# Five RMS norms of a decoder step: one product of ones and a root on 272 columns in place of small sums, small roots and a spread

## The chip, the cores and the metric

The kernel runs on one core of a Trainium2 chip. A core has a matmul engine (TensorE, PE in the profile; its weight loads are shown as PEld), three engines for elementwise work (VectorE = DVE, ScalarE = ACT, GpSimd = POOL), and queues that start DMAs (SP's, ACT's and POOL's). Each engine works through its own queue in order; semaphores hold an instruction until what it reads is there and what it overwrites is free. The metric is the device time of one execution, in microseconds (us).

## What is computed

One layer of a hybrid decoder, for a prompt of 512 tokens and 32 sample tokens (8 sequences of 4), 544 tokens in all, with a model width of 1024, in float32. With the parts that matter here spelled out:

```
def _rmsnorm(x, g):
    return x * rsqrt(mean(x * x, axis=-1) + 1e-6) * g

def _layer(x, ...):
    m = mixer(_rmsnorm(x, norm_mix_pre), ...)       # RG-LRU and attention branches, then @ W_out
    x = x + _rmsnorm(m, norm_mix_post)
    f = conv_ffn(_rmsnorm(x, norm_ffn_pre), ...)    # @ W_up, conv over 3 positions, gelu gate, @ W_down
    x = x + _rmsnorm(f, norm_ffn_post)
```

## The kernel before

The activations lie turned: a tile holds 128 channels on its partitions and the tokens along its columns, so the width of 1024 is eight tiles (index c), and a sum over the width is a sum over partitions and over eight tiles. The tokens come in two halves, of 272 and 272 columns (HALF2) up to the FFN's start and of 256 and 288 (HALF) in the down projection. Half a = 0 is worked on first.

Each float32 operand of a large product is split into a high and a low part (names ending in H and L, weights wh and wl), and a product is made of three matmuls for each 128 channels. ScalarE writes the high parts, VectorE subtracts for the low parts. The weights are split as they arrive (wh_e, wl_e for the first FFN products).

A norm in the middle of the kernel, in norm_chain(a, acc), goes like this. While a projection's tiles come out of PSUM, ScalarE squares them and VectorE adds the squares up in one tile acc of [128 channels, 272 tokens]. Then:

- stats: acc itself is loaded as weights, in three pieces of 128 columns, against a single column of ones. The result, a PSUM tile pst with one token on each partition and three columns, holds the sums. newton_rstd takes the root of it on ScalarE (AF.Sqrt from a table), the reciprocal and one Newton step on VectorE, all on 3 columns.
- diag: VectorE multiplies the identity by each of the three columns, which gives diagonal tiles (dg).
- spread: a product of ones [128 x 128] with dg puts each token's factor on all 128 partitions (PSUM tile rep, 272 columns).
- then, for each c, VectorE multiplies the tile by its gain (a column of pv) and by rep.

This is done for the norm behind the out-projection (tiles named ..._m0 and ..._m1) and, once x1 = x + that norm and its squares (accx) are there, for the norm ahead of the FFN (..._f0, ..._f1). The normalised tiles are then split into b11, b21 (half 0) and b12, b22 (half 1), the operands of the FFN's first products (pq). The last norm, finish_b ("o1"), does the same for the second half of the FFN's output ft; its squares lie in two tiles, acc and sq7, so there are six small products. Token tiles 0 and 1 of the output take another way, with tokens on partitions: newton_rstd on one column (rstd), and for tile 1 a root written out at the kernel's end.

The order of the work. TensorE's order is that of the program, throughout. A clock `now` counts steps of products: half of an out-projection or one FFN product is 0.5. A generator started with start_at runs until its next `yield t` and goes on t later on that clock; what it emits then stands behind the products emitted so far. NORM_TICKS, YS, YA, YB and FB are such pauses: YS between the sums and diag, YA and YB between diag and spread, NORM_TICKS between the first norm's work and the sums of the second, FB ahead of the spread in finish_b. For VectorE, ScalarE and POOL the order is written out by hand too, except between the end of the mixer and the FFN's main loop (some 370 to 450 us), where a scheduler orders them by priority and readiness; norm_chain raises the priority there (tc.high_priority). In the last stage ScalarE's and VectorE's order is again that of the program, and POOL's is not.

ScalarE's functions come from tables. A one-element activation (warm) ahead of a stage makes the table load happen early: at the kernel's start, at the end of the mixer (L1153) and near the end of the down projection (L1926).

Of the kernel before, what the change touches and what calls it, by code (L numbers as in the profile page):

```python
# [56 lines left out]
NORM_TICKS = (3.5, 1)  # L57
# [3 lines left out]
YA = (0.5, 0.5)  # L61
YB = (0.5, 0.5)
EARLY = 4
PLAIN = 6
FB = (1.0,)
# [58 lines left out]
def hawk_step(ctx, tc, I, O):  # L124
# [249 lines left out]
    act.activation(warm, epst, AF.Sqrt)  # L374
# [27 lines left out]
    pv = keep.tile([P, 96], F32, name="pv")  # L402

# [10 lines left out]
    G_PRE, G_POST, G_FPRE, G_FPOST, C_W, C_B, C_BR, C_BI, C_LAM = 0, 8, 16, 24, 32, 64, 72, 80, 88  # L414
# [738 lines left out]
    act.activation(warm, epst, AF.Sqrt)  # L1153
# [3 lines left out]
    def stats(acc, nch, nm, more=None):  # L1157

        ps = PX("pst_" + nm)
        for z in range(nch):  # L1160
            mm(ps[:, z:z + 1], acc[:, z * P:(z + 1) * P], ones[:, 0:1], z == 0, more is None and z == nch - 1)
        for z in range(nch if more is not None else 0):
            mm(ps[:, z:z + 1], more[:, z * P:(z + 1) * P], ones[:, 0:1], False, z == nch - 1)
        st = SM("nst_" + nm, [P, 3, 4], "nst")
        v, r, s_ = (st[:, z, :nch] for z in range(3))
        newton_rstd(r, v, s_, ps[:, :nch])
        return r

    def diag(r, n, nm):
        dg = T("dg_" + nm)  # L1170
        for z in range((n + P - 1) // P):
            w = min(P, n - z * P)
            dve.tensor_scalar(dg[:, z * P:z * P + w], ident[:, :w], r[:, z:z + 1], None, ALU.mult)
        return dg

    def spread(dg, n, nm):

        rep = PX("rep_" + nm)
        mm(rep[:, :n], ones, dg[:, :n], True, True)
        return rep  # L1180

    def sq_sum(acc, src, n, first, nm):
        if first:
            act.activation(acc[:, :n], src, AF.Square)
            if n % P:
                pool.memset(acc[:, n:n + P - n % P], 0.0)
# [53 lines left out]
    def norm_chain(a, acc):  # L1240
        lo, hi = HALF2[a]
        n = hi - lo
        nch = (n + P - 1) // P
        with tc.high_priority(offset=HP):
            r = stats(acc, nch, f"m{a}")
            yield YS[a]
            dg = diag(r, n, f"m{a}")
        yield YA[a]
        with tc.high_priority(offset=HP):
            rep = spread(dg, n, f"m{a}")  # L1250
# [6 lines left out]
            for c in range(0 if a else 8):  # L1257
                m_ = mt[c][:, lo:hi]
                stt(m_, m_, pv[:, G_POST + c:G_POST + c + 1], rep[:, :n], ALU.mult, ALU.mult)
                pool.tensor_tensor(out=x1_(c), in0=x1_(c), in1=m_, op=ALU.add)  # L1260
                sq_sum(acc2, x1_(c), n, c == 0, f"x{a}_{c}")
            for g in range(6 if a else 0):
                for c in range(2 * g, 2 * g + 2) if g < 4 else ():
                    m_ = mt[c][:, lo:hi]
                    stt(m_, m_, pv[:, G_POST + c:G_POST + c + 1], rep[:, :n], ALU.mult, ALU.mult)
                    pool.tensor_tensor(out=x1_(c), in0=x1_(c), in1=m_, op=ALU.add)
                for c in range(2 * g - 3, 2 * g - 1) if 1 <= g < 6 else ():
                    if 0 <= c < 8:
                        sq[c] = acc2 if c == 0 else T(f"sq_x{a}_{c}")
                        act.activation(sq[c][:, :n], x1_(c), AF.Square)  # L1270
                        if c == 0 and n % P:
                            pool.memset(acc2[:, n:n + P - n % P], 0.0)
# [4 lines left out]
        with tc.high_priority(offset=HP):  # L1277
            r = stats(acc2, nch, f"f{a}")
            yield YS[a]
            dg = diag(r, n, f"f{a}")  # L1280
        yield YB[a]
        with tc.high_priority(offset=HP):
            rep = spread(dg, n, f"f{a}")

            def normed(c, dst):
                stt(dst, x1[c][:, lo:hi], pv[:, G_FPRE + c:G_FPRE + c + 1], rep[:, :n], ALU.mult, ALU.mult)
# [521 lines left out]
    def finish_b(acc):  # L1808
# [3 lines left out]
        dg = diag(stats(acc, 3, "o1", sq7), n, "o1")  # L1812
        yield FB[0]
        rep = spread(dg, n, "o1")
        for c in range(8):
            f_ = ft[c][:, lo:hi]
            stt(f_, f_, pv[:, G_FPOST + c:G_FPOST + c + 1], rep[:, :n], ALU.mult, ALU.mult)
# [103 lines left out]
    for c in range(8):  # L1921
# [3 lines left out]
        if c == 5:  # L1925
            act.activation(warm, epst, AF.Sqrt)  # L1926
# [35 lines left out]
    act.activation(s_, ssq[:, 1, 2:3], AF.Sqrt, scale=1.0 / D, bias=b_)  # L1962
# [4 lines left out]
    dve.reciprocal(r, s_)  # L1967
# [40 lines left out]
```

## Time and profile before

| | us |
|---|---|
| three runs | 977.36, 978.94, 979.18 (median 978.94) |
| profiled execution | 977.74 |
| its span in the profile | 976.0 |
| granted TensorE clock | 0.998 of full speed |
| busy in the span | PE 967.6, PEld 959.9, DVE 758.6, ACT 551.0, POOL 168.8 |

The span lies inside the execution's time: 1.74 us are outside it. A busy TensorE isn't TensorE at its peak, since matmuls overlap and their ends are modelled. The chain that ended last, followed back from the end of the span, tells which engine's work set the end.

### The profile page before, as it was taken

The numbers are of one execution on the slowest core, as the hardware profiler recorded it, in microseconds if no ns is written. First come the engines' busy times: TensorE is split into PE (matmuls) and PEld (weight loads), VectorE is DVE, ScalarE is ACT, GpSimd is POOL, SyncE is SP. The second block draws the span as 40 slices with busy tenths as digits, with TensorE's granted clock in tenths as the row PEclk, the third lists the DMA queues.
The fourth block names the chain that finished last, engine by engine and source line by source line (L and its number), as shares of the span: only waits on it lengthen the run. The fifth ranks groups of instructions, "written<-read, shape, count | busy, mean of one in ns | idle before, by whom it ended". The sixth has DMA issues, their size and how long they took to land.

```text
span 976.0 us, 20122 instructions
## 1 busy us (share of the span) xinstructions
PE 967.6 (99%) x7668; PEld 959.9 (98%) x7668; DVE 758.6 (78%) x1632; ACT 551.0 (56%) x1344; POOL 168.8 (17%) x288
## 2 busy tenths in 40 slices
PE   9999999999999999999999999999999999999997
PEld 8999999999999999999999999999999999999996
DVE  5777888857858555699967888787888888888875
ACT  6544443467476435556767665655555555556652
POOL 2152000003306331230011111101011101011024
PEclk9999999999999999999999999999999999999999
DMA  7875535632334547136157585858586766768612
GB/s 217 237 239 163 151 88 147 161 93 87 109 113 126 175 121 189 45 122 184 39 114 189 126 191 129 184 137 177 140 179 157 169 156 160 166 140 221 201 30 92
DMA packets 234204, 143.07 MB, mean 147 GB/s; under 512 B 25012, under 2 KB 218940, under 8 KB 234076
## 3 DMA queue, kind: packets, MB, share of 16 engines
q1 hardware_dynamic: 224300, 120.21, 43.9%
q0 software_dynamic: 9696, 19.42, 11.9%
q10 hardware_dynamic: 112, 2.17, 0.6%
q8 instruction: 60, 0.98, 0.4%
q14 instruction: 36, 0.29, 0.1%
HBM read 115.59 MB, written 15.17 MB: 134 GB/s over the span
## 4 chain that ended last, share of the span: by engine, by line
PE 97%; DVE 1%; ACT 1%; DMA 0%; issue 0%; SPq 0%; POOL 0%; ACTq 0%; POOLq 0%
PE pmin L165 20%; PE pmdn L165 19%; PE pux L1536 16%; PE puy L1536 8%; PE pq L1536 7%; PE pmout L165 5%; PE pmlo L165 5%; PE pmao L165 5%; PE puz L1536 4%; PE pg L165 1%; PE pvp L165 1%; PE psc L165 1%; PE ptok L165 1%; DMA pt<-pd 0%; PE ps_warm L165 0%; PE pm_first L165 0%
## 5 line engine op out<-in xcount | busy, mean ns | idle before, releaser
L165 PE MATMUL pmin<-hH,wh_in 128*128 128x256 f32 (+1 forms) x568 | 164.0, 291 | 0.0
L165 PE MATMUL pmin<-hL,wh_in 128*128 128x256 f32 (+1 forms) x568 | 162.5, 288 | 0.0
L165 PE MATMUL pmin<-hH,wl_in 128*128 128x256 f32 (+1 forms) x568 | 159.3, 288 | 0.0
L165 PE MATMUL pmdn<-fH,wh_dn 128*128 128x256 f32 (+1 forms) x448 | 129.3, 289 | 0.0
L165 PE MATMUL pmdn<-fH,wl_dn 128*128 128x256 f32 (+1 forms) x448 | 129.2, 288 | 0.0
L165 PE MATMUL pmdn<-fL,wh_dn 128*128 128x256 f32 (+1 forms) x448 | 129.0, 288 | 0.0
L165 PEld LDWEIGHTS pmin<-hH,wh_in 128*128 128x128 f32 x568 | 107.3, 189 | 1.2 <-issue 1.0
L165 PEld LDWEIGHTS pmin<-hL,wh_in 128*128 128x128 f32 x568 | 107.4, 189 | 0.1
L165 PEld LDWEIGHTS pmin<-hH,wl_in 128*128 128x128 f32 x568 | 104.8, 188 | 0.2 <-issue 0.2
L177 DVE SCALAR_TENSOR_TENSOR uc<-u,fv,uc 128x560 f32<-128x560 f32 x128 | 102.0, 797 | 1.7 <-ACT uc L1567 1.1
L165 PEld LDWEIGHTS pmdn<-fL,wh_dn 128*128 128x128 f32 x448 | 84.4, 188 | 0.0
L165 PEld LDWEIGHTS pmdn<-fH,wl_dn 128*128 128x128 f32 x448 | 84.4, 188 | 0.0
L165 PEld LDWEIGHTS pmdn<-fH,wh_dn 128*128 128x128 f32 x448 | 84.4, 188 | 0.0
L1664 ACT COPY u<-pux 128x272 f32<-128x272 f32 x52 | 20.1, 386 | 84.4 <-PE pux L1536 84.2
L168 DVE TENSOR_TENSOR u<-puy,u 128x240 f32<-128x240 f32 (+2 forms) x78 | 24.6, 343 | 48.8 <-PE puy L1536 32.2
L174 DVE TENSOR_TENSOR ft<-ft,pmdn 128x256 f32<-128x256 f32 (+1 forms) x104 | 45.0, 434 | 15.7 <-PE pmdn L165 15.7
L283 ACT ACTIVATE wh_in<-raw_in 128x512 fp32r<-128x512 f32 x70 | 42.2, 625 | 20.7 <-issue 11.0
L290 DVE TENSOR_TENSOR wl_in<-raw_in,wh_in 128x512 fp32r<-128x512 f32 x70 | 47.8, 694 | 1.0 <-ACT wh_in L283 1.0
L1567 ACT ACTIVATE uc<-u,fv 128x560 f32<-128x560 f32 x64 | 48.2, 755 | 0.0
L779 ACT ACTIVATE s<-s,st 128x256 f32<-128x256 f32 (+1 forms) x32 | 15.2, 475 | 53.8 <-DVE st L776 46.1
L168 DVE TENSOR_TENSOR wl_dn<-raw_dn,wh_dn 128x512 fp32r<-128x512 f32 x56 | 38.3, 685 | 3.8 <-ACT wh_dn L1485 3.8
L1474 POOL DMA_DIRECT2D raw_up_s<-raw_up_s x26 | 22.4, 861 | 95.8 <-DMA raw_up_s<-raw_up__11277 5.4
(761 smaller groups left out, 3388.5 us busy)
## 6 DMA issues: line engine op xcount, KB each, us to landing
raw_in<-in_w_in_dram SPq DMA_DIRECT2D x35, 512.0 KB
raw_dn<-in_w_down_dram SPq DMA_DIRECT2D x56, 256.0 KB
raw_up_s<-in_w_up_dram SPq DMA_DIRECT2D x25, 512.0 KB
raw_up_s<-raw_up_s POOLq DMA_DIRECT2D x26, 256.0 KB, 5.3
raw_ao<-in_w_attn_o_dram SPq DMA_DIRECT2D x8, 512.0 KB
raw_lo<-in_w_lru_o_dram SPq DMA_DIRECT2D x8, 512.0 KB
raw_out<-in_w_out_dram SPq DMA_DIRECT2D x8, 512.0 KB
pd<-pb SPq DMA_DIRECT2D x12, 256.0 KB
```

The lines of the kernel that those rows point to most:

```text
L165: pe.matmul(out, l, r, start=start, stop=stop)
L168: dve.tensor_tensor(out=out, in0=a, in1=b, op=ALU.subtract)
L174: dve.tensor_tensor(out=out, in0=a, in1=b, op=ALU.add)
L177: dve.scalar_tensor_tensor(out=out, in0=a, scalar=s_, in1=b, op0=op0, op1=op1)
L283: act.activation(hl[0], raw, AF.Copy)
L290: (eng or dve).tensor_tensor(out=hl[1], in0=raw, in1=f32(hl[0]), op=ALU.subtract)
L779: act.activation(s3[:, j, :], s3[:, j, :], AF.Exp, bias=ng[:, j:j + 1], accum_out=sm[:, j:j + 1])
L1474: pool.dma_start(out=w["p4"], in_=w["p2"], accum_op=ALU.add)
L1536: pe.matmul(ps[:, :HN], w, x, start=start and k == 0 and i == 0, stop=stop and k == 3 and i == 2, skip_group_check=True)
L1567: act.activation(yt[j][:, 0:FLATU], u[:, 0:FLATU], AF.Copy, scale=fv[:, j:j + 1])
L1664: act.copy(e[nm_], z)
```

## The change

All five norms of the middle and the end (m0, m1, f0, f1, o1) take one way: a product of ones [128 x 128] with the tile of squares puts the sum of each token on all 128 partitions at once (272 columns, 288 at the end, where the two tiles of squares are accumulated). ScalarE takes the reciprocal root of it from a table (Abs_reciprocal_sqrt) on all columns and squares it; VectorE makes a Newton step in two multiplications on all columns, whose result is -2 times the factor and is left in the same PSUM tile. The gains are multiplied by -0.5 once, at the start (pvn). The Newton steps on few columns (the first norms, token tiles 0 and 1) take the same table function and lose their reciprocal. POOL's zeroing of the columns beyond 272 goes. The pauses YA and YB go, NORM_TICKS[0] rises from 3.5 to 4, so that the second product of half 0 stands where its sums stood; for half 1 a pause of 0.5 is kept between root and Newton step; FB falls from 1.0 to 0.5.

```diff
-NORM_TICKS = (3.5, 1)
+NORM_TICKS = (4, 1)
 YS = (0.5, 0.5)
-YA = (0.5, 0.5)
-YB = (0.5, 0.5)
-FB = (1.0,)
+FB = (0.5,)
...
-    act.activation(warm, epst, AF.Sqrt)
+    act.activation(warm, epst, AF.Abs_reciprocal_sqrt)
...
     def newton_rstd(r, v, s_, sq):
-        act.activation(s_, sq, AF.Sqrt, scale=1.0 / D, bias=epst)
+        act.activation(r, sq, AF.Abs_reciprocal_sqrt, scale=1.0 / D, bias=epst)
         dve.tensor_scalar(v, sq, 1.0 / D, EPS, ALU.mult, ALU.add)
-        dve.reciprocal(r, s_)
...
+        dve.tensor_scalar(pvn, pv[:, 8:32], -0.5, None, ALU.mult)
...
-    def stats(acc, nch, nm, more=None):
-        ps = PX("pst_" + nm)
-        for z in range(nch):
-            mm(ps[:, z:z + 1], acc[:, z * P:(z + 1) * P], ones[:, 0:1], ...)
...
-        newton_rstd(r, v, s_, ps[:, :nch])
-    def diag(r, n, nm):
...
-    def spread(dg, n, nm):
-        rep = PX("rep_" + nm)
-        mm(rep[:, :n], ones, dg[:, :n], True, True)
+    def total(accs, n, nm):
+        ps = PX("pst_" + nm)
+        for z, acc in enumerate(accs):
+            mm(ps[:, :n], ones, acc[:, :n], z == 0, z == len(accs) - 1)
+        return ps
+
+    def root_table(ps, n, nm):
+        y, w = (T(f"{x}_{nm}")[:, :n] for x in ("ry", "rw"))
+        act.activation(y, ps[:, :n], AF.Abs_reciprocal_sqrt, scale=1.0 / D, bias=epst)
+        act.activation(w, y, AF.Square, scale=1.0 / 32.0)
+        return y, w
+
+    def root_newton(ps, n, y, w):
+        stt(w, ps[:, :n], D * EPS, w, ALU.add, ALU.mult)
+        stt(ps[:, :n], w, -3.0, y, ALU.add, ALU.mult)
+        return ps
...
     def norm_chain(a, acc):
         with tc.high_priority(offset=HP):
-            r = stats(acc, nch, f"m{a}")
-            yield YS[a]
-            dg = diag(r, n, f"m{a}")
-        yield YA[a]
+            ps = total([acc], n, f"m{a}")
+        yield YS[a]
         with tc.high_priority(offset=HP):
-            rep = spread(dg, n, f"m{a}")
+            yw = root_table(ps, n, f"m{a}")
+            if a:
+                yield 0.5
+            rep = root_newton(ps, n, *yw)
...
-                stt(m_, m_, pv[:, G_POST + c:G_POST + c + 1], rep[:, :n], ALU.mult, ALU.mult)
+                stt(m_, m_, pvn[:, G_POST + c:G_POST + c + 1], rep[:, :n], ALU.mult, ALU.mult)
...
     def finish_b(acc):
-        dg = diag(stats(acc, 3, "o1", sq7), n, "o1")
+        ps = total([acc, sq7], n, "o1")
         yield FB[0]
-        rep = spread(dg, n, "o1")
+        rep = root_newton(ps, n, *root_table(ps, n, "o1"))
...
-    act.activation(s_, ssq[:, 1, 2:3], AF.Sqrt, scale=1.0 / D, bias=b_)
+    act.activation(r, ssq[:, 1, 2:3], AF.Abs_reciprocal_sqrt, scale=1.0 / D, bias=b_)
...
-    dve.reciprocal(r, s_)
```

More of the change, by code (lines that the diff above doesn't have):

```diff
@@ L402, in hawk_step @@
     pv = keep.tile([P, 96], F32, name="pv")
+    pvn = keep.tile([P, 24], F32, name="pvn")
     pw = PM("ps_warm")
@@ L1152, in hawk_step @@
         step(("lo", c), L, a, lo_done(c), target=upto(("lo", min(c, 6) if a == 0 else c), a, 2))
-    act.activation(warm, epst, AF.Sqrt)
+    act.activation(warm, epst, AF.Abs_reciprocal_sqrt)
     mixer.close()
-    def stats(acc, nch, nm, more=None):
+    def total(accs, n, nm):
         ps = PX("pst_" + nm)
-        for z in range(nch):
[L1161 to L1165, printed above, removed]
-        newton_rstd(r, v, s_, ps[:, :nch])
-        return r
-    def diag(r, n, nm):
[L1170 to L1174, printed above, removed]
-    def spread(dg, n, nm):
-        rep = PX("rep_" + nm)
-        mm(rep[:, :n], ones, dg[:, :n], True, True)
-        return rep
+        for z, acc in enumerate(accs):
[10 more added lines that the diff above has]
+        return ps
     def sq_sum(acc, src, n, first, nm):
@@ L1264, in norm_chain @@
                     m_ = mt[c][:, lo:hi]
-                    stt(m_, m_, pv[:, G_POST + c:G_POST + c + 1], rep[:, :n], ALU.mult, ALU.mult)
+                    stt(m_, m_, pvn[:, G_POST + c:G_POST + c + 1], rep[:, :n], ALU.mult, ALU.mult)
                     pool.tensor_tensor(out=x1_(c), in0=x1_(c), in1=m_, op=ALU.add)
@@ L1277, in norm_chain @@
         with tc.high_priority(offset=HP):
[L1278 to L1281, printed above, removed]
+            ps = total([acc2], n, f"f{a}")
+        yield YS[a]
         with tc.high_priority(offset=HP):
-            rep = spread(dg, n, f"f{a}")
+            yw = root_table(ps, n, f"f{a}")
+            if a:
+                yield 0.5
+            rep = root_newton(ps, n, *yw)
             def normed(c, dst):
-                stt(dst, x1[c][:, lo:hi], pv[:, G_FPRE + c:G_FPRE + c + 1], rep[:, :n], ALU.mult, ALU.mult)
+                stt(dst, x1[c][:, lo:hi], pvn[:, G_FPRE + c:G_FPRE + c + 1], rep[:, :n], ALU.mult, ALU.mult)
             def first(k2):
```

12 lines of the change are left out of this document (4 added, 8 removed).

## The prediction

> **What bounds the kernel now.** First the page: how busy each engine is, at what granted clock, and which engine carries the chain that ended last.
>
> ```profile
> PE 967.6 (99%) x7668; PEld 959.9 (98%) x7668; DVE 758.6 (78%) x1632; ACT 551.0 (56%) x1344; POOL 168.8 (17%) x288
> PEclk9999999999999999999999999999999999999999
> PE 97%; DVE 1%; ACT 1%; DMA 0%; issue 0%; SPq 0%; POOL 0%; ACTq 0%; POOLq 0%
> ```
>
> TensorE is the bound: 97% of the chain are matmuls, one behind the other, at full clock in every slice. A matmul taken off its queue shortens the run by the time it held the queue, as long as VectorE, ScalarE and the DMAs keep up. So two questions decide: how long do the five norm sums hold TensorE, and does what stands behind them come in time when TensorE gets there earlier?
>
> Second the chain in order of time, at the norms (start, length, engine, tile, count). "m" is the norm behind the out-projection, "f" the one ahead of the FFN, each for half a = 0 and a = 1; "o" is the last.
>
> ```profile
> 396.11 0.56 PE pst_m L165 x6
> 396.67 3.12 PE pmout L165 x24
> 399.79 0.46 PE rep_m L165 x2
> 400.25 10.56 PE pmout L165 x84
> 410.81 0.56 PE pst_f L165 x6
> 411.37 3.11 PE pmout L165 x24
> 414.48 0.46 PE rep_f L165 x2
> ...
> 420.98 0.80 PE pst_m L165 x6
> 421.78 3.12 PE pq L1536 x24
> 424.89 0.46 PE rep_m L165 x2
> ...
> 437.43 0.83 PE pst_f L165 x6
> 438.26 3.12 PE pq L1536 x24
> 441.38 0.46 PE rep_f L165 x2
> ...
> 949.24 1.24 PE pst_o L165 x12
> 950.48 2.96 PE pmdn L165 x24
> 953.43 0.49 PE rep_o L165 x2
> 953.92 2.79 PE ptok L165 x12
> ```
>
> The reader is to see that each norm stands on TensorE's path twice: as sums (pst, six instructions for three products with one column each) and 24 matmuls later as the spread (rep, two instructions for one product of 272 columns). An undisturbed matmul of 272 columns takes 10.56/84 = 0.126 us, so 24 should take 3.02; behind each pst they take 3.11 or 3.12. So a sum costs its piece and 0.10 more of the matmuls behind it. Behind rep there is no such extra: the 84 of 10.56 are the ones behind it.
>
> **TensorE's part of the change.** The sums and the spread go; one product of ones with the 272 squared sums comes at the place of the sums. It has the form of the spread word for word (ones as the weights, 272 plain float32 columns), so I price it by rep's row, 0.46: what goes as spread comes back as product, and the net gain is what the sums cost.
> - m and f of half 0: 0.56 + 0.10 and 0.56 + 0.09, together 1.31.
> - m and f of half 1: the same instructions took 0.80 and 0.83. The excess over 0.56, 0.24 and 0.27, I read as a wait for the squares' last addition, which the product meets too. I count only 0.66 for each: 1.32.
> - o: twelve instructions, 1.24 + 0.10, and a spread of 0.49 go; two products (acc and sq7, 288 columns) come, 2 x 0.49 = 0.98. Gain 0.85.
>
> Sum 1.31 + 1.32 + 0.85 = 3.48. Bounds: if the two waits of half 1 vanish as well, 4.0; the other end is the next paragraph.
>
> One rule speaks against the size. The Trainium skill, "TensorE: Matmul & The Clock Gate", section "Back-to-back issue gap", gives a matmul of 1 to 64 columns an issue floor of about 25 ns. By that figure six instructions would hold TensorE 0.15 us and the gain would be an estimated 4 x 0.15 + 12 x 0.025 + 0.49 - 0.98 = 0.4 us, no measurable change. The trace does not agree: six took 0.56, 93 ns each, and twelve took 1.24. The same section says that a stream in which each matmul loads its weights runs slower than the isolated gap, and here every product of pst loads another 128 columns of acc. Rival 2 is what would follow if the rule held.
>
> **The way from sum to factor, on ScalarE and VectorE.** It goes beside TensorE's other matmuls and costs nothing unless a product comes late. The timeline shows the first use of each factor and what is late next (start, length, engine, line, what; in brackets the idle time ahead and what ended it):
>
> ```profile
> 400.29 1.72 DVE L177 SCALAR_TENSOR_TENSOR mt<-mt,pv,rep_m 128x272 f32<-128x272 f32 x4 [0.74 <-PE rep_m L165]
> 408.94 0.43 DVE L174 TENSOR_TENSOR accx<-accx,sq_x 128x272 f32<-128x272 f32 x1
> 415.06 1.72 DVE L177 SCALAR_TENSOR_TENSOR h2f<-x,pv,rep_f 128x272 f32<-128x272 f32 x4 [0.71 <-PE rep_f L165]
> 425.39 0.91 DVE L177 SCALAR_TENSOR_TENSOR mt<-mt,pv,rep_m 128x272 f32<-128x272 f32 x2 [1.18 <-PE rep_m L165]
> 435.44 1.94 DVE L174 TENSOR_TENSOR accx<-accx,sq_x 128x272 f32<-128x272 f32 x4
> 437.89 0.69 DVE L168 TENSOR_TENSOR wl_e<-raw_up__5874,wh_e 128x512 fp32r<-128x512 f32 x1
> 441.96 1.72 DVE L177 SCALAR_TENSOR_TENSOR h2t<-x,pv,rep_f 128x272 f32<-128x272 f32 x4 [0.30 <-PE rep_f L165]
> 446.50 1.53 DVE L168 TENSOR_TENSOR b22L<-h2t,b22H 128x544 fp32r<-128x544 f32 x2
> 448.58 0.29 PE L1536 MATMUL pq<-b22L,wh_e 128*128 128x272 f32 x1
> 953.96 0.94 DVE L177 SCALAR_TENSOR_TENSOR ft<-ft,pv,rep_o 128x288 f32<-128x288 f32 x2 [0.99 <-PE rep_o L165]
> 960.40 1.57 POOL L1818 TENSOR_TENSOR ft<-ft,x1r 128x288 f32<-128x288 f32 x2
> 962.55 1.03 PE L1829 MATMUL pyo<-ident,ft 128*128 128x128 f32 x8
> ```
>
> VectorE's load is in the table of stretches, here the one that holds half 1 (length, then the busy time of TensorE, its weight loads, VectorE, ScalarE and POOL, the clock, the DMAs):
>
> ```profile
> 421.00:446.00 25.00, 24.97 (x195) 24.59 (x196) 23.02 (x53) 13.61 (x30) 7.70 (x8) 1.00 0.65 200
> ```
>
> And the prices of the new operations are in the groups (count, busy time in all, mean ns of one):
>
> ```profile
> L454 ACT ACTIVATE hH<-ps_tb,pv 128x288 fp32r<-128x288 f32 x8 | 3.4, 511 | 1.1 <-PE ps_tb L529 1.1
> L1189 ACT ACTIVATE sq_x<-x 128x272 f32<-128x272 f32 x7 | 3.0, 432 | 2.8 <-POOL x L1260 2.8
> L177 DVE SCALAR_TENSOR_TENSOR mt<-mt,pv,rep_m 128x272 f32<-128x272 f32 x16 | 7.2, 488 | 1.9 <-PE rep_m L165 1.9
> L1153 ACT ACT_TABLE_LOAD x1 | 1.3, 1283 | 0.0
> ```
>
> From the end of the sums to the first use of the factor it is now 396.67 to 400.29, 411.37 to 415.06, 421.78 to 425.39, 438.26 to 441.96 and 950.48 to 953.96: 3.5 to 3.7 us, and at all five places VectorE's last wait is for the spread, which stands 24 matmuls behind. The new way: a root over 272 columns from PSUM with a pointer as bias (0.50, from the 511 ns of the 288-column row with a pointer), its Square (0.43), two Newton steps (2 x 0.49), all in series, with some 0.1 at each of four hand-overs: about 2.3 us. It needs no second visit to TensorE. So the way gets about 1.3 shorter, and TensorE's stretch only 0.66 shorter: the cover grows by some 0.7 at each norm, if the queues take the new operations at once. Four covers:
> - The f product of half 0 (410.81) reads accx, whose last addition ends at 408.94 + 0.43 = 409.37: cover 1.4.
> - The f product of half 1 waits already: accx ends at 435.44 + 1.94 = 437.38, and the product starts at 437.43. Cover none.
> - The second b22L ends at 446.50 + 1.53 = 448.03; its first matmul starts at 448.58. Cover 0.55.
> - The last adds on POOL end at 960.40 + 1.57 = 961.97; the turn of ft starts at 962.55. Cover 0.58. There the pause between sum and factor becomes half of what it was (FB), so ft's multiplications are emitted one product earlier, ahead of the first token product's addition.
>
> VectorE's order between 396 and 450 is found by a scheduler, not written by hand, so I can't read it from the code. In the window of half 1 VectorE is busy 23.02 of 25.00, and the weight splits (wl_e, 0.69) share its queue. A Newton step that waits there for the Square holds the splits behind it; split low parts that come late hold TensorE. Bounds for the way: 2.3 with free queues; three splits ahead of it, 3 x 0.69 = 2.1, make 4.4. I take the near end, because at four of the five places VectorE is idle for 0.7 us or more ahead of the first use, so it has room there.
>
> **Edits that I cost at nothing.** The reciprocals of the first norms and the one copy of gains times -0.5 are operations on a few columns, behind TensorE's continuous start. POOL's zeroing of the accumulators' ends goes; no row above waits for it. At the end the last root's reciprocal goes (a single column), but the chain ends in copies of pyo, which wait for TensorE, so it is not what ends last. The product's PSUM tile lives from the sum to the last use, where two tiles lived one after the other; no piece of the chain waits for a PSUM tile now. Were these covers gone, each would cost about its own few tenths. No DMA is added or moved by name; the loads that follow the norms' steps in SP's queue come as much earlier as TensorE does.
>
> **Sum.** 977.74 - 3.5 = 974.2 for the profiled execution (span 976.0 and 1.74 around it). It lies 1.20 below the median of the three runs; the same difference on the median: 978.94 - 3.5 = **975.4**. About 0.2%, 2.0 us, is what a measurement of this kernel can tell from no change.
>
> **Rivals.**
> 1. Half 1 loses part. If the way there is not shorter (as at f of half 1 today, where splits run ahead of the small steps), the f product comes 0.66 late and b22L 0.66 - 0.55 = 0.11: the gain shrinks to 2.7, 976.2. With one split more ahead of each it shrinks by 1.4 further, 977.6, no change. For: 23.02 of 25.00 busy. Against: 1.18 idle at 425.39, which the change gives back.
> 2. The change doesn't do what it says on TensorE. Were the sums' 0.56 + 0.10 not the price of six instructions but that of changing to plain float32 and back, the product would pay it too, on top of what rep shows, and the gain would sink towards 0: 978.9. A sum that holds TensorE hardly at all gives the same. Against: twelve instructions cost 1.24, just over twice the 0.56 of six, so the price goes by the instruction; and rep changes number format as well and has nothing behind it. The page's floor named above would put this case at an estimated 978.5.
> 3. Slower: Newton's steps stand far back in VectorE's queue at every norm. If the way grows by D over today's, the four places above lose (D + 0.66 - 1.4) + (D + 0.66) + (D + 0.66 - 0.55) + (D + 0.85 - 0.58) = 4 D + 0.3. It decides from 5.5 lost, D = 1.3, a way of about 5 us: four splits ahead of Newton each time. With five splits D = 2.1, loss 8.7, and the time is 984.1. For it: nothing but the unknown order and the 23.02 us. Against: the steps are emitted ahead of the uses and with a raised priority.
> 4. A table switch inside the way. One load is 1.283 us. Were Square not in the same table as the new root, each norm would pay two, 2.57: the way would be 4.9, D = 1.2, the loss 5.1 and the time 980.5, at the edge of measurable. The rows of before show Squares and copies between the norms' roots with no load after the one at L1153, but for the old root's table. The Trainium skill, "ScalarE: Activation LUTs", section "Table sets: the hidden batching unit", says that cheap functions such as copy and abs stand in every set; it does not list Square there, and no trace here shows the new root's set.
>
> **How the numbers follow.** Forecast (3.0 to 4.0 gained, 974.9 to 975.9) 0.62; more than that, with the waits of half 1 gone and the rest of the FFN's start eased, 0.05; rival 1 0.15, half of it still over 2.0 gained; rival 2 0.09; rival 3 0.05; rival 4 0.04, half of it slower. Faster 0.62 + 0.05 + 0.07 = 0.74; slower 0.05 + 0.02 = 0.07, with 0.01 for the unnamed 0.08; the rest, 0.18, the same. The range holds the forecast, the greater gain and rival 1: its low end is 4.0 gained and 1.2 for the spread of the runs (median against profiled execution), 973.7; its high end is rival 1's worse end, 977.6.
>
> **What the profile after would show.** Right: one piece of 0.46 at each of four norms and about 0.98 at the last, no piece 24 matmuls behind, 24 matmuls in 3.02 behind the product; the first use of the factor about 2.3 us behind the product; no more table loads than now. Wrong: issue or a wait ahead of the f product of half 1 or of the first b22 matmul that grows over 0.3; Newton steps behind wl_e; ACT_TABLE_LOAD rows next to a root. If the chain is no longer TensorE between 396 and 450, the forecast has failed there.

## The result, and the profile after

| | us |
|---|---|
| before, six runs | 977.36 to 979.18, median 978.40 |
| after, six runs | 973.95 to 974.46, median 974.29 |
| ratio after to before | 0.9959, 95% interval 0.9948 to 0.9971 |
| span of the profiled execution | 976.0 before, 972.2 after |

The change gains about 4.0 us (2.8 to 5.1 by the interval); 3.5 were forecast. The time itself is 1.1 under the forecast 975.4, half of it because the forecast stood on the median of three runs of before, 978.94, and that of six is 978.40. The gain comes out near the forecast, but not by the forecast's terms: one of its four 0.66s isn't there, and steps that it put at nothing make up for part of that.

The page of the kernel after, the same three lines as before: engines, granted clock, and the chain by engine.

```profile
PE 963.0 (99%) x7634; PEld 955.2 (98%) x7634; DVE 756.3 (78%) x1599; ACT 553.9 (57%) x1349; POOL 167.9 (17%) x282
PEclk9999999999999999999999999999999999999999
PE 94%; DVE 3%; ACT 1%; issue 0%; DMA 0%; POOL 0%; SPq 0%; DVEq 0%; ACTq 0%; POOLq 0%
```

TensorE is busy 4.6 us less, and the span is 3.8 shorter. VectorE's share of the chain went from 1% to 3%: about 2% of 972, nearly 20 us more, in which the chain runs over VectorE and no longer along TensorE's queue. Where these lie is seen in the chain in order of time (start, length, engine, tile, line, count; "..." stands for lines left out, here and in all that follows):

```profile
395.53 0.46 PE pst_m L163 x2
395.99 13.57 PE pmout L163 x108
409.56 0.46 PE pst_f L163 x2
410.02 1.51 PE pmout L163 x12
...
412.32 0.48 ACT ry_f L1167
...
414.32 1.72 DVE h2f L175 x4
...
419.22 0.45 DVE acc L172
...
419.71 0.74 PE pst_m L163 x2
...
435.10 0.45 DVE accx L172
...
435.59 0.72 PE pst_f L163 x2
...
946.51 0.97 PE pst_o L163 x4
947.48 2.84 PE pmdn L163 x24
```

The reader is to see four things. The product of ones takes 0.46 at m0 and f0 and 0.97 at o1, as priced, and no piece for a spread follows: at m0 108 matmuls stand in one piece of 13.57, 0.126 each. At m1 and f1 the product takes 0.74 and 0.72, where the sums took 0.80 and 0.83: it still waits for the last addition, and how long the starts of the matmuls tell (group 2). From 411.53, where the 12 matmuls of 1.51 end, to 419.71 the chain no longer runs on TensorE. It goes over the root (ry_f), VectorE's first use of f0's factor (h2f) and its addition of token squares (acc) to the product of m1; among the lines left out are a copy on ScalarE ahead of the root, the square, Newton's two steps and the two b11L. And from 420.45 to 435.59 it is off TensorE again: from m1's sum over its root, its Newton steps, weight splits (wl_e) and the additions of accx to the product of f1.

The table below is worked out from the starts of all of TensorE's matmuls: for each one that both kernels have, its start after less its start before, read off ahead of and behind each norm. The column of m1 takes in the stretch from f0 to m1's product, where matmuls stall as well. For instance the matmuls just behind the spread of m0 come 1.24 earlier, those ahead of m0 0.58: the step at m0 is -0.66.

| step of the shift, us | start to m0 | m0 | f0 | m1 | f1 | to o1 | o1 | total behind o1 |
|---|---|---|---|---|---|---|---|---|
| forecast | 0 | -0.66 | -0.65 | -0.66 | -0.66 | 0 | -0.85 | -3.48 |
| after | -0.58 | -0.66 | -0.70 | +0.03 | -0.60 | -0.22 | -0.86 | -3.59 |
| after, second execution (run e11_after_again) | -0.38 | -0.66 | -0.70 | +0.01 | -0.57 | -0.18 | -0.86 | -3.34 |

Four norms give what was forecast, to within 0.1. The gain of m1 is missing in both executions. The steps at the start and in the long FFN stretch were forecast as nothing and, together 0.6 to 0.8, make up for it by their size.

### The profile page after: what moved, and what is told of

Read it like the earlier page. It is cut to its first block, busy times and chain, and to the rows that moved or that the text cites. A ratio compares the mean times of both kernels' runs of the same rounds, so it can differ in the third digit from the quotient of the medians.

```text
span 972.2 us, 20023 instructions
## 1 busy us (share of the span) xinstructions
PE 963.0 (99%) x7634; PEld 955.2 (98%) x7634; DVE 756.3 (78%) x1599; ACT 553.9 (57%) x1349; POOL 167.9 (17%) x282
## 4 chain that ended last, share of the span: by engine, by line
PE 94%; DVE 3%; ACT 1%; issue 0%; DMA 0%; POOL 0%; SPq 0%; DVEq 0%; ACTq 0%; POOLq 0%
PE pmin L163 20%; PE pmdn L163 19%; PE pux L1527 16%; PE puy L1527 8%; PE pq L1527 6%; PE pmlo L163 5%; PE pmao L163 5%; PE pmout L163 4%; PE puz L1527 4%; PE pg L163 1%; PE pvp L163 1%; PE psc L163 1%; PE ptok L163 1%; DVE wl_e L166 0%; DMA pt<-pd 0%
```

## The experiments

Theory A is that of the prediction: TensorE's queue carries the time, a sum costs by its instructions, and what lies between sum and factor is covered as long as the queues take it at once. Its rivals are named with each run. "Before" in each group is the kernel before, run on the same chip: 977.67 in the first, 977.77 in the second, 978.09 in the third. In group 3 the kernel after was not run beside the others; "above the kernel after" there is against its 974.21 of group 2, and the shifts of the matmuls, read from just ahead of m0 to the end, give the same differences.

### Group 1: what each part is worth

**The roots on few columns alone** (kernel before, with only the new root for the first norms and the small sums, without reciprocal):

```diff
-        act.activation(s_, sq, AF.Sqrt, scale=1.0 / D, bias=epst)
+        act.activation(r, sq, AF.Abs_reciprocal_sqrt, scale=1.0 / D, bias=epst)
...
-        dve.reciprocal(r, s_)
```

> The kernel of before with only the small roots changed: the table's reciprocal root in place of root and reciprocal on the few columns of the first norms, the middle norms and the token tiles. Theory A (the gain is the time that the norm sums held TensorE's queue): TensorE's work is unchanged, so 0 to -0.2 us, at most the 0.15 us of a reciprocal where the second group of first norms is waited for at 34 us. Rival B (a good part of the gain comes from roots that are ready earlier): -0.6 us or more, with the shift of 0.6 us that the changed kernel showed by 35 us seen here too, and again at each norm between 396 and 442 us.

Measured 977.77, ratio 1.0001 (0.9993 to 1.001). In its profile the matmuls ahead of m0 come 0.68 earlier, but this is gone at the end, where they come 0.14 earlier. By the time these edits cost and bring nothing, as forecast. But one part of the 0.68 is real: at the product that spreads the factors of the first norms (ps_rep, 34 us) the shift steps by 0.13 to 0.17 in each of the four kernels with the new small roots (this one, the next, and both executions of the kernel after), and by nothing in the one below that keeps the old roots. A reciprocal of 0.18 is gone there from VectorE's queue ahead of that product. The rest of the 0.68 lies in the first 10 us, where executions differ by 0.1 to 0.6.

**The new way at the last norm only**, on top of that, with the shorter pause FB:

```diff
-        dg = diag(stats(acc, 3, "o1", sq7), n, "o1")
+        ps = total([acc, sq7], n, "o1")
         yield FB[0]
-        rep = spread(dg, n, "o1")
+        rep = root_newton(ps, n, *root_table(ps, n, "o1"))
```

> As the kernel with the small roots alone, and the last norm in the new way too (two products of ones, root and Newton step on 288 columns, the shorter pause); the four norms between 396 and 442 us stay as in before. Theory A: -0.85 us against the kernel with the small roots alone, all of it between the start of the sums at 949 us and the token products: one piece of about 0.97 us in place of 1.24 + 0.10 and 0.49. Rival B: the factor is ready about 1.4 us earlier, so POOL's last additions and the output rows come that much earlier and the end moves by more than 1 us. No shift between 396 and 442 us under either.

Measured 976.74, ratio 0.9992 (0.9983 to 1.0), 1.03 under the run with the roots alone. Its chain at the last norm:

```profile
948.85 0.97 PE pst_o L165 x4
949.82 2.84 PE pmdn L165 x24
```

The sums' 1.24 with 2.96 behind them, and the spread's 0.49, have become 0.97 with 2.84 behind. Against the kernel before, the matmuls' shift steps by 0.87 here and by nothing between m0 and o1. The term of 0.85 stands.

**The small sums made twice** (kernel before, each of the three products of 128 columns with a column of ones issued a second time into unused columns):

```diff
+        for z in range(nch):
+            mm(ps[:, 8 + z:9 + z], acc[:, z * P:(z + 1) * P], ones[:, 0:1], True, True)
```

> The kernel of before with the three small products of each norm's sums made twice, the first time into columns that nobody reads. Theory A: six more instructions hold TensorE by 0.56 us at each of the five norms, +2.8 us in all. If most of a sum's price is the change of number format and back (the prediction's second rival), the second helping is cheap: under 0.15 us a norm, +0.7 us or less. If TensorE has room there (rival B), nothing.

Measured 981.01, ratio 1.0037 (1.0024 to 1.0051), +3.3 us. The chain at m0 and at o1:

```profile
396.01 1.23 PE pst_m L165 x12
397.25 3.14 PE pmout L165 x24
...
951.85 1.91 PE pst_o L165 x18
```

Six more instructions make 0.56 into 1.23, while the 24 matmuls behind still take 3.14. The five steps are 0.70, 0.66, 0.67, 0.68 and 0.66. So the price is that of the instructions, 0.11 us each, and is paid again for each set: the second rival (a change of format, paid once) falls. The floor of 25 ns that the prediction took from the Trainium skill, "TensorE: Matmul & The Clock Gate", section "Back-to-back issue gap", would make the 30 added instructions an estimated 0.75 us; this run shows 3.3.

**The product of ones made twice** (kernel after):

```diff
         ps = PX("pst_" + nm)
+        mm(ps[:, :n], ones, accs[0][:, :n], True, True)
         for z, acc in enumerate(accs):
```

> The changed kernel with the product of ones made twice at each of the five norms (at the last norm the first of its two). Theory A: each further product holds TensorE by its row, 0.46 us and 0.49 at the last: +2.3 us against the changed kernel, or -1.8 against the kernel of before. Where the way behind the product is already late for TensorE (the norm m of half 1), it comes 0.46 later as well, so no relief there. If a format change were the price, +0.5 or less. Rival B: TensorE's queue time is not what counts, so about 0.

Measured 976.59, ratio to before 0.999 (0.9982 to 0.9999); 2.3 over the kernel after. The pieces are 0.92 for two products:

```profile
395.72 0.92 PE pst_m L163 x4
...
948.61 1.46 PE pst_o L163 x6
```

At m1 and f1, where the wait is in the piece, it is 1.20 and 1.19. Five steps of 0.45 to 0.48. The product's price of 0.46 holds at all five places. Both TensorE prices of the sum are thereby measured; what is missing at m1 is not a price.

### Group 2: where m1's gain went, and what the way costs

The kernel after shows a candidate. ScalarE's timeline at f0 (in brackets the idle time ahead and what ended it):

```profile
411.55 0.40 ACT L1344 ACTIVATE mt<-pmout 128x272 f32<-128x272 f32 x1 [2.31 <-PE pmout L163]
...
412.32 0.47 ACT L1167 ACTIVATE ry_f<-pst_f,epst 128x272 f32<-128x272 f32 x1
```

The sum is there at 410.02, but the root starts at 412.32: it stands in ScalarE's queue behind a copy of out-projection tokens that waits until 411.55 for TensorE. ScalarE is idle for 2.31 us, the last 1.5 of them with the sum at hand. TensorE pays for it at m1:

```profile
418.13 0.29 PE L1527 MATMUL pq<-b11H,wh_e 128*128 128x272 f32 x1
418.54 0.39 PE L1527 MATMUL pq<-b11L,wh_e 128*128 128x272 f32 x1
...
419.15 0.29 PE L1527 MATMUL pq<-b11H,wl_e 128*128 128x272 f32 x1
419.71 0.72 PE L163 MATMUL pst_m<-acc,ones 128*128 128x272 f32 x2 [0.27 <-DVE acc L172]
...
420.40 0.29 PE L1527 MATMUL pq<-b11L,wh_e 128*128 128x272 f32 x1
```

Matmuls start 0.126 apart. The one on b11L starts 0.41 behind its predecessor, a stall of 0.28, and the next (418.77) 0.23 behind that, another 0.10. From the last matmul ahead of the product to the second behind it are 1.25, two distances of 0.126 and 0.46 of product leave 0.54 of waiting for the addition. Before, the same stretch was

```profile
420.67 0.28 PE L1536 MATMUL pq<-b11H,wl_e 128*128 128x272 f32 x1
...
421.85 0.29 PE L1536 MATMUL pq<-b11L,wh_e 128*128 128x272 f32 x1
```

1.18, less two distances and the sums' 0.66: 0.27 of waiting. So m1 lost 0.28 + 0.10 at b11L and 0.27 more waiting at its product: the whole of its 0.66, as the table has it.

**The kernel after once more**, to share a chip with the next three.

> The changed kernel unaltered, so that the next three stand beside it on one chip. 974.0 to 974.5 us is expected from its six runs so far (973.95 to 974.46). In the shift of its matmuls against the kernel before, the steps were m0 -0.6, f0 -0.7, m1 about 0 (0.6 gained and lost), f1 -0.6, o1 -0.9. What this run tells: whether the loss at m1 is in the program or in one execution. If in the program, the root of f0 starts again some 2.3 us after the product's end, behind the copy that waits for TensorE, one fused product waits about 0.3 for the second b11L, and the product at m1 waits about 0.3 for the addition. If it was one execution, m1 shows -0.6 and the waits are gone.

Measured 974.21, ratio 0.9963 (0.995 to 0.9975). The second execution's row in the table above: the loss at m1 is in the program, not in one execution.

**f0's root early** (kernel after; at half 0 the root is emitted right behind the product, so at f0 it stands ahead of that copy; the same edit is made at m0, where it moves nothing):

```diff
-        yield YS[a]
-        with tc.high_priority(offset=HP):
+            if a:
+                yield YS[a]
             yw = root_table(ps, n, f"f{a}")
-            if a:
-                yield 0.5
+        yield 0.5
+        with tc.high_priority(offset=HP):
             rep = root_newton(ps, n, *yw)
```

> The changed kernel with the two norms' table roots of half 0 put into ScalarE's queue right behind their product, so that at f0 the root stands ahead of the copy of mixed tokens that waits for TensorE; m0 keeps its order. Theory A (the gain of m1 was lost because f0's root stood 1.5 to 2.3 us behind that copy, which made b11L and through VectorE's queue the last addition of m1 late): the way at f0 falls from 4.3 to about 2.9 us, the stall of 0.28 before the second product on b11L goes, the wait of m1's product falls back towards nothing, m1's step becomes -0.4 to -0.6, and the time is 0.4 to 0.6 us under the changed kernel. Rival B (VectorE's work of half 1 sets the addition's end, and the root's place doesn't matter): the way at f0 shortens, but the addition still ends where it did, and the time is within 0.2 of the changed kernel. Rival C (the copy, now behind the root and the square, gives up its PSUM tile 0.9 us later, and the projection behind it waits): 0.3 to 0.9 us slower than the changed kernel.

Measured 974.31, ratio to before 0.9965 (0.9953 to 0.9978): no gain over the 974.21 of the kernel after. Its chain around m1:

```profile
410.26 7.53 PE pmout L163 x60
...
417.82 0.40 ACT mt L1344
418.22 0.56 ACT b21H L1287
...
418.80 0.35 DVE b21L L166
...
419.44 0.44 DVE acc L172
...
419.93 0.74 PE pst_m L163 x2
```

VectorE's first use of f0's factor:

```profile
412.32 0.91 DVE L175 SCALAR_TENSOR_TENSOR h2f<-x,pvn,pst_f 128x272 f32<-128x272 f32 x2
```

The first half of the theory was right and wasn't enough. The first use is 2.06 behind the sum instead of 4.30 (410.02 to 414.32), and the stall at b11L is gone. But the product of m1 starts as late as ever: the addition it needs (acc) takes the last token square, whose tile was copied at 417.82, and behind that copy ScalarE does b21H first, and VectorE a b21L. What was two waits is one wait (the idle time ahead of the product in the profile grew from 0.27 to 0.65).

**The square made four times** at each norm (kernel after; three more squares of 0.43 on the way, TensorE unchanged):

```diff
-        act.activation(w, y, AF.Square, scale=1.0 / 32.0)
+        for _ in range(4):
+            act.activation(w, y, AF.Square, scale=1.0 / 32.0)
```

> The changed kernel with the square on ScalarE made four times at each of the five norms: three more instructions of about 0.43, so the way from sum to factor is about 1.3 us longer, at every norm. Theory A (TensorE's queue is the bound, and the way lies under it with the cover that the prediction named: 1.4 at f0, none at f1, 0.55 at b22L): at m0 and o1 some 0.0 to 0.4 us, at f0 about 1 to 1.3 because its cover is used up by the detour already, at f1 about 0.7 to 1.3; together 2 to 3 us above the changed kernel. Rival B (the way is on the path everywhere, and the gain came from the shorter way, not from TensorE's instructions): five times 1.3, 6.5 us above. Rival C (the way is hidden everywhere): within 0.3 of the changed kernel.

In its profile the way from the sum to the first use of the factor is 1.8, 1.55, 1.4, 1.3 and 1.4 longer at m0, f0, m1, f1 and o1. Measured 979.84, ratio to before 1.0021 (1.0012 to 1.003): 5.6 above the kernel after, where theory A said 2 to 3 and "on the path everywhere" 6.5. TensorE's own waits in this kernel (engine, line, releaser: us in total, times, longest):

```profile
PE pst_f L163 <- DVE accx L172: 1.8, 2, 1.4
PE pq L1528 <- DVE b11L L166: 1.2, 2, 0.8
...
PE pq L1528 <- DVE wl_e L166: 0.7, 1, 0.7
...
PE pq L1528 <- DVE b22L L166: 0.4, 1, 0.4
```

By the shift against the kernel after, m0's way costs 1.7 (at f0's product), f0's 1.0 (at b11L), m1's 1.4 (1.0 of it at a matmul that waits for a weight split, wl_e, and only 0.2 at f1's product), f1's 1.0 (0.3 at b12L, 0.7 at b22L), and o1's 0.3; some 0.3 are small steps along the FFN. At f0, f1 and o1 that is about what theory A said. It missed at m0, which it took for covered, and at m1, which it didn't name. m1's cost goes by a path that is no wait for the factor at all: the squares stand on ScalarE ahead of the high part of a weight split, VectorE is idle for 2.07 until that is there, and the splits behind come late to TensorE. This gave theory A2: behind m0, f0, m1 and f1 the way and TensorE's queue come to an end at about the same time, and the later of the two counts.

**The way taken out** (kernel after; root, square and Newton's two steps are left out, and the sum itself, scaled in the gains, multiplies the tokens):

```diff
-            rep = root_newton(ps, n, *yw)
+            rep = ps
```

> The changed kernel without root, square and the two Newton operations at the five norms: the sum itself, scaled by a constant in the gains, multiplies the tokens, so the output isn't the normalised one and only the time is read. The way from sum to factor is about 1.9 us shorter at each norm, by the four operations and their handovers, and ScalarE has ten instructions less and VectorE ten less. Theory A (TensorE's own instructions carry the time; of the way only what shows as a wait of TensorE is left to gain: the stall of 0.28 at b11L, about 0.3 at m1's product, the short waits behind f1): 0.6 to 1.2 us under the changed kernel, with m1's step back at -0.6. Rival B (the way is on the path at every norm): 5 times 1.9, up to 9 us under. Rival C (nothing of the way shows): within 0.3 of the changed kernel, and m1's loss stays.

Measured 973.59, ratio to before 0.9957 (0.9943 to 0.9971): only 0.6 under the kernel after, at the low end of theory A's 0.6 to 1.2, though the way is 2.0 to 4.2 shorter at each of the five places (at f1 1.1 of it is left, elsewhere 0.1 or less). The shift steps are -0.73 at m1 and -0.36 at f1, nothing at m0, f0 and o1; 0.5 of it is lost again along the FFN, which no wait explains. So the kernel after stands near the knee: a way 1.3 to 1.8 longer costs most of that at four of the five places, a shorter one brings m1's lost gain and little more.

### Group 3: theory A2, both sides

**The square made twice** (kernel after; one more square of 0.43 on the way):

```diff
+        for _ in range(2):
             act.activation(w, y, AF.Square, scale=1.0 / 32.0)
```

> The changed kernel with the square on ScalarE made twice at each of the five norms: the way from sum to factor is 0.44 us longer, so about as long as before the change, while TensorE's own instructions stay as few. This asks how much of the gain of 4.0 hangs on the shorter way. Theory A2 (what four squares showed: TensorE's queue and the way end about together at m0, f0, m1 and f1, with cover left only at o1): about 0.3 to 0.45 at each of the four, nothing at o1; 1.2 to 1.8 us above the changed kernel, 975.4 to 976.0. Rival A1 (the covers of the prediction, 1.4 at f0 and 0.55 in front of b22L, are there, and four squares only overran them): 0.1 to 0.7 above. Rival B (the whole gain is the way's): 4 above, as slow as before.

Measured 975.65, ratio to before 0.9975 (0.9967 to 0.9984): 1.4 above the kernel after, in theory A2's range. In its profile the way is 3.6 at m1 and f1, just what it was before the change, 4.8 at f0, 4.3 at m0 (the scheduler put wh_e between the squares there) and 2.5 at o1. And by place it isn't 0.3 to 0.45 at each of four: it is 0.5 at f0 and at m1 and 0.1 at m0 and f1, with 0.25 more along the FFN, which no norm explains (the table below). So at m0 and f1 some cover is left.

**An unread product** behind each sum (kernel after; one more product of ones 12 instructions behind the sum's, so TensorE's queue is longer and the way is not):

```diff
             yw = root_table(ps, n, f"m{a}")
+            filler(acc, n, f"m{a}")
...
+        pf = PX("fil_" + nm)
+        mm(pf[:, :n], ones, acc[:, :n], True, True)
```

> The changed kernel with one more product of ones at each norm, 12 instructions behind the sum's in TensorE's queue; nobody reads it. It lengthens TensorE's queue and not the way, and stands where the product for the spread factor stood before. Theory A2 (TensorE's queue and the way end about together; longer queue means longer time, and gives the way the same cover): 5 x 0.46 = 2.3, less the 0.3 of the wait at b11L that it covers: 1.7 to 2.4 us above the changed kernel, 976.0 to 976.7. Rival B (the way decides, and the filler lies beside it): 0 to 0.6 above.

Measured 976.12, ratio to before 0.9981 (0.9972 to 0.9989): 1.9 above. In its chain TensorE carries half 1 again, and the product of f1 no longer waits:

```profile
420.79 0.70 PE pst_m L163 x2
...
423.00 0.46 PE fil_m L163 x2
423.46 13.54 PE pq L1534 x108
437.00 0.46 PE pst_f L163 x2
```

The fillers of m0, f0, m1, f1 and o1 cost 0.45, 0.43, 0.09, 0.47 and 0.52: the one of m1 lies in what was f1's wait.

**Both edits together.**

> Both edits: the square twice, and the unread product behind the sum. Theory A2 (at each norm the later of queue and way counts): the filler's 0.46 gives the cover that the second square's 0.44 needs, so the two together cost what the dearer one costs alone, 2.0 to 2.7 us above the changed kernel. Rival D (the costs add, because the way ends in other engines' queues and not in a wait of TensorE): the sum of the two runs, 3.2 to 4.2 us above.

Measured 976.62, ratio to before 0.9988 (0.9979 to 0.9997): 2.4 above. Alone they cost 1.4 and 1.9, together 2.4: more than the dearer one alone, less than the sum of 3.3. The places tell why. The steps of the shift against the kernel after, between the same matmuls in all three:

| us above the kernel after | m0 | f0 | m1 | f1 | along the FFN | o1 |
|---|---|---|---|---|---|---|
| square twice | 0.1 | 0.5 | 0.5 | 0.1 | 0.25 | 0.0 |
| unread product | 0.45 | 0.4 | 0.1 | 0.5 | 0.0 | 0.5 |
| both | 0.45 | 0.5 | 0.45 | 0.5 | 0.0 | 0.5 |

At each norm both together cost what the dearer one costs there, and that one is not the same at every norm. Added work on TensorE gives the longer way its cover: at each place the later one counts, as theory A2 has it, and the costs don't add.

**The last token square straight from PSUM** (on the kernel with f0's root early):

```diff
+            if c == 7:
+                sq_sum(acc, ps[:, :n], n, False, f"wo{a}_{c}")
             act.activation(mt[c][:, lo:hi], ps[:, :n], AF.Copy)
-            sq_sum(acc, mt[c][:, lo:hi], n, c == 0, f"wo{a}_{c}")
+            if c < 7:
+                sq_sum(acc, mt[c][:, lo:hi], n, c == 0, f"wo{a}_{c}")
```

> The kernel with f0's root early, and with the last token square ahead of each m-norm read straight from PSUM instead of from the copied tile, so that it stands ahead of the copy in ScalarE's queue; at half 1 the square then stands ahead of the last b21H copy, and its addition ahead of the last b21L in VectorE's queue. Theory A2 (with f0's root early, m1's product waited only for that addition, whose square stood behind the mt copy and a b21H copy of 0.56): at m1 the product starts when TensorE reaches it, 0.3 to 0.7 earlier; at m0 up to 0.4 if its product waits for the same chain, nothing if not; 0.3 to 0.8 us under the changed kernel, 973.4 to 973.9. Rival E (the last b21L, now behind the addition, makes a fused product wait as long): within 0.2 of the changed kernel.

Measured 973.31 (973.12 to 973.47), ratio to before 0.9954 (0.9942 to 0.9966): 0.9 under the kernel after (0.3 to 0.8 were expected), the fastest kernel of this study. ScalarE, VectorE and TensorE at m1:

```profile
417.78 0.40 ACT L1181 ACTIVATE sq_wo<-pmout 128x272 f32<-128x272 f32 x1 [1.27 <-PE pmout L163]
...
418.27 0.44 DVE L172 TENSOR_TENSOR acc<-acc,sq_wo 128x272 f32<-128x272 f32 x1
...
418.95 0.29 PE L1530 MATMUL pq<-b11H,wl_e 128*128 128x272 f32 x1
419.08 0.62 PE L163 MATMUL pst_m<-acc,ones 128*128 128x272 f32 x2
...
419.66 0.29 PE L1530 MATMUL pq<-b11L,wh_e 128*128 128x272 f32 x1
```

The addition ends at 418.71, ahead of the product's place; from 418.95 to 419.66 are 0.71, which is 0.46 and two distances. The shift against the kernel after steps by -0.92 at m1 and by less than 0.1 at every other place. That is the lost 0.66 and the wait of 0.27 that was there before. What took m1's gain is thereby shown: the order on ScalarE and VectorE, in two places. The first edit alone brought nothing, both together the whole; the second without the first was not run.

## Why the forecast was right, and where not

- **The sums' price** (0.56 + 0.10 for six instructions): right. Made twice they cost 0.66 to 0.70 at each norm.
- **The product's price** (0.46, and 0.98 at o1): right, 0.46 and 0.97; made twice, 0.45 to 0.48 more.
- **The net steps**: right at m0 (0.66), f0 (0.70), f1 (0.60) and o1 (0.86). **Wrong at m1**: 0.66 forecast, nothing measured.
- **The way of about 2.3.** The prices of the operations were right: 0.48 for the root (0.50 forecast), 0.43 for the square, 0.44 and 0.45 for Newton (0.49 each), by the groups after (count, busy, mean ns of one):

```profile
L1167 ACT ACTIVATE ry_f<-pst_f,epst 128x272 f32<-128x272 f32 x2 | 1.0, 480 | 0.5 <-PE pst_f L163 0.5
L1168 ACT ACTIVATE rw_f<-ry_f 128x272 f32<-128x272 f32 x2 | 0.9, 432 | 0.1
L175 DVE SCALAR_TENSOR_TENSOR rw_f<-pst_f,rw_f 128x272 f32<-128x272 f32 x2 | 0.9, 438 | 0.4 <-ACT rw_f L1168 0.4
L175 DVE SCALAR_TENSOR_TENSOR pst_f<-rw_f,ry_f 128x272 f32<-128x272 f32 x2 | 0.9, 450 | 0.1
```

The 0.1 at each hand-over stood on no row of before; at o1 an operation follows the one it waits for by 0.03 to 0.04. So the way was 2.0 at o1 (947.48 to 949.52 below), where the queues are free. But it was 3.1 at m0 (395.99 to 399.13) and 4.3 at f0, and 3.1 at m1 and 3.2 at f1, both with Newton behind weight splits on VectorE (wl_e), as the first rival had it. The lines for m0, f1 and o1:

```profile
399.13 1.31 DVE L175 SCALAR_TENSOR_TENSOR mt<-mt,pvn,pst_m 128x272 f32<-128x272 f32 x3
...
437.92 0.69 DVE L166 TENSOR_TENSOR wl_e<-raw_up__5918,wh_e 128x512 fp32r<-128x512 f32 x1
438.53 0.43 DVE L175 SCALAR_TENSOR_TENSOR rw_f<-pst_f,rw_f 128x272 f32<-128x272 f32 x1
...
949.52 0.94 DVE L175 SCALAR_TENSOR_TENSOR ft<-ft,pvn,pst_o 128x288 f32<-128x288 f32 x2
```

The step that failed is "the cover grows by some 0.7 at each norm, if the queues take the new operations at once", taken because "VectorE is idle for 0.7 us or more ahead of the first use". That idle time said that VectorE waited for the spread. It said nothing of ScalarE, whose queue now holds two operations of 272 columns at each norm where it held one of 3, and which at f0 waited for TensorE with the root behind: 4.3 of way there instead of 2.3. In place of 1.3 shorter, the way got 0.5 shorter at m0 and m1, 0.45 at f1 and 1.4 at o1, and 0.6 longer at f0. And the list of four covers lacks what f0's way has to be in time for, b11L and m1's last addition: those are where the 0.66 went (0.38 at b11L, 0.27 at m1's product). The prediction's own sign for this came true, though its time was met: between 411.53 and 435.59 the chain is mostly not TensorE's, and "the forecast has failed there".
- **The first rival** (half 1 loses part) therefore happened in its result, at one norm: the way that lengthened was f0's, and it was m1's product that came late. At b22L the loss that it feared did not come; no wait for b22L stands among the waits of the kernel after.
- **The covers.** "None" at f1 was right. The 1.4 at f0 did not hold as a cover: with three more squares m0's way cost 1.7 at f0's product, more than the edit itself, since the orders shift with it (the ScalarE half of a weight split, wh_e, now stands among the squares, and two additions of acc among VectorE's last of accx). The cover at b22L was there: in the kernel after the second b22L ends 0.42 ahead of its first matmul (445.64 and 446.06), a way 0.4 longer cost 0.1 there, and one 1.3 longer cost 1.0 behind f1. So was the cover at the end: 0.3 of 1.3 came through at o1.
- **Waits of half 1**: that the product meets them too was right at f1; at m1 the wait doubled, from 0.27 to 0.54.
- **Costs of nothing**: the reciprocal of the first norms' second group was worth 0.13 to 0.17, too little to see in the time. The rest of the step ahead of m0 (0.38 to 0.58 in all) lies in the first 10 us, where executions differ; its cause stays open.
- **Second rival** (change of format): fell by the doubled sums. **Third** (slower, Newton far back): a way of 4.3 at f0 came near to its 5, at one place. **Fourth** (a table switch): fell; there are twelve loads before and after, at the same places of the program, and none between the norms of 396 to 442 us or at the last norm. The one ahead of the last norm:

```profile
L1917 ACT ACT_TABLE_LOAD x1 | 1.3, 1283 | 0.0
```

- **The total.** The five norms gave 2.8 by the shift instead of 3.5. The other 0.6 to 0.8 of the 3.3 to 3.6 are the reciprocal and small steps at the start and along the FFN, of the size by which two executions of one kernel differ. The forecast's nearness to the measured 4.0 owes something to them: that part is luck. And what the forecast treated as free cover was part of the gain: with TensorE's saving kept and one square more on the way, 1.4 of it is gone (0.6 of that at m0 and f0, whose ways are then longer than before the change).

## What to carry to other kernels

When an instruction is taken off a saturated engine, follow the chain beside it as well: the gain lasts only as far as that chain ends earlier too, and once both end together, the later one counts at each place. An idle engine ahead of a step shows room on that engine alone; look in every queue of the chain for an instruction that waits for the bound engine itself, since whatever is queued behind it waits too. Put the small operation that others wait for ahead of such a copy, and where removing one wait brings nothing, look at once for the next in the same queue order. List what each factor has to be in time for before counting covers, also what only shares a queue with it.

## What was not expected of the hardware

Products with a single column, each with weights of its own, are dear for TensorE: 0.11 us for each plain float32 instruction (3.3 us for 30 more), about as much as the 0.126 between two matmuls of 272 columns of the split kind. A product of ones over 272 plain float32 columns, 0.46, costs less than three products over one column, 0.66, and leaves the sums on all partitions.
